# The low-rank decay columns of a fused decoder layer move into the first indexer group

## The chip, the cores and the metric

One core of a Trainium2 chip runs the whole layer as one program. Its engines are TensorE (PE, matrix products, with PEld for its weight loads), VectorE (DVE), ScalarE (ACT), GpSimd (POOL) and SyncE (SP, which here issues the loads). Each engine takes its own instructions in the order in which the program gives them and waits for the others by semaphores. The metric is the device time of one execution in microseconds (us); the kernel before took 1889.96, 1892.20 and 1893.36 us in three runs, so a median of 1892.2 us.

## The reference, cut to what matters

All is float32: 256 tokens, a model width of 2048, one layer. A normed and modulated input h is multiplied by one wide matrix, and the columns of the result are split among the branches:

```python
proj = h @ w_in                                # 2048 x 16984
(g_q, g_k, g_v, g_r, g_lr, d_q, d_k, d_v, i_q, i_k, i_w, gate_a, gate_b) = split(proj)
# widths: 1024 1024 2048 2048 16 2048 2048 2048 512 64 8 2048 2048
log_g = log_sigmoid(g_lr @ gla_gate_up + gla_gate_bias) / 16    # decay of the linear attention
o_a   = gla_chunked(q_a, k_a, v_a, log_g)      # 4 heads; then norm, gain, silu(g_r)
score = sum_h i_w[h] * relu(i_q[h] . i_k / 8)  # indexer: 8 heads of 64, the best 64 keys per query
o_b   = softmax attention over the chosen keys # 16 heads of 128
x     = x + g1 * ((sigmoid(gate_a) * (o_a @ w_branch_gla) + sigmoid(gate_b) * (o_b @ w_branch_dsa)) @ w_merge_out)
x     = x + g2 * swiglu(norm(x)); return final_norm(x)
```

The change concerns g_lr, 16 columns of the projection, and the indexer's 584 columns (i_q, i_k, i_w).

## The kernel before, in words

Weights stream through the core once. A *chunk* (class Mm) is up to four row tiles of 128 of a weight matrix and up to 512 columns. SP loads it into one of three raw buffers. Then `pre_mm` splits it in halves: ACT rounds a half to the float32r part `hi` (L303) and DVE subtracts it from the original, which gives the exact rest `lo` (L305). `main` multiplies: for each row tile and each of two token tiles of 128, three products, activations' `hi` by weights' `hi` (L345), `hi` by `lo` (L346) and `lo` by `hi` (L347). A chunk of four row tiles is 24 products. A *group* is the four chunks of one set of columns; its result is in two PSUM tiles, which the group's `evac` copies out.

`run` goes through the list `items`. After each chunk's products it records the split of the chunk that comes two later (`pres`), then, behind a group's last chunk, the copies out of PSUM, and then it lets three *threads* each take a step, as long as a credit lasts that grows by 3.6 us for a chunk of 512 columns: `qa` is the gated linear attention (GLA), `qb` the transposes of queries and keys, `qc` the indexer's scoring, top-k search and the softmax attention. A step's small products stand on PE behind the chunk, its other work behind the chunk's split on the other engines. Where a later group needs a thread's result, the thread is *drained*: its remaining steps are recorded at once. All engines keep the order so recorded; there is no other scheduler.

Around the change the list is: the first products (q, k, v, r of GLA) in four slices of the depth; `init_end` (rotary tables, buffers of the later stages); the low-rank chunk (class Lr); two indexer groups of 292 columns; then the groups named in `ORDER = "d0 a0 a1 d1 a2 a3 d2 y0 y1 d3 y2 y3"`, in which a *d* is three groups (queries, keys, values of four attention heads), an *a* a gate and a *y* a branch product.

The low-rank chunk is 2048 x 128 columns, of which 16 are needed. Its weights are the stationary operand: for each row tile one product with 512 columns (both parts of h, L327) and one with 256 (L328), 32 in all, so the result is already transposed, ranks by tokens. `lr_evac` adds the two halves (L591, L592) and starts the GLA thread:

```python
            act.copy(lrT[0:16, 0:S], ps[0:16, 0:S])
            dve.tensor_tensor(lrT[0:16, 0:S], lrT[0:16, 0:S], ps[0:16, S:2 * S], ALU.add)
            state["lr"] = True
            qa.add(gla())
```

The GLA thread first transposes q and k (L613), multiplies the low-rank rows by the gate matrix (L628), takes logarithms and a running sum (L646, L650). Then, for each of 4 heads and 4 pairs of block sizes, `prep` has POOL subtract (L663), ACT take exponentials (L667) and DVE multiply (L672), and the next step has PE multiply (L693 to L705, L679). At a head's end come the product with the values (L732 to L734), a scaling by DVE (L737), a sum of squares on ACT (L738), a power on POOL (L218, L219) and a scaling (L766). After the last head 32 transposes (L753), four to a PSUM tile, are split by ACT (L758) and DVE (L759). `psum_aux` has three buffers. `attend(g)` drains GLA when g is 1. The indexer's columns are copied out by `idx_evac` (L797 to L800); the rotation is `rope` on POOL (L779 to L784), L816 and L826 transpose the indexer's queries and keys, L839 to L847 score, L857 and L858 search the top keys. The transposes of attention queries and keys are L944, the first product of an attention head is L973.

Of the kernel before, what the change touches and what calls it, by code (L numbers as in the profile page):

```python
# [16 lines left out]
S = 256  # L17
# [6 lines left out]
RAW_BUFS = 3          # raw chunks of weights in flight  # L24
EARLY_RAWS = 3        # and more of them while the working tiles of later stages are not there yet
HL_BUFS = 4           # halves of split chunks
AHEAD = 2             # chunks split ahead of their products
INIT_KTS = (4, 4, 4, 4)    # row tiles of the slices of the first products
ADA_DONE = 8          # the group of a slice before which the next slice's modulation is loaded and then applied
ADA_LEAD = (0, 2, 4)  # groups by which each slice's pieces of it start early  # L30
MID = 2               # row tile of the last chunk before which the first token tile's norm goes on
# The second norm's steps (512 columns, token tile) after the first two, with p for a half of a split,
# and the steps done before each row tile of the chunks that read them.
NORM_STEPS = "p 01 11 p p 20 21 30 31"
NORM_DONE = "0000 1233 3333 4557 7777 7777"
SLOT = 3.6            # vector engine time for the threads beside a chunk, in us
# [9 lines left out]
class Mm:  # L46
    """A chunk of a weight matrix: nk row tiles of 128, nc columns, for a group of products.

    With defer, the second token tile waits until a later chunk with by_token has done the first one.
    With home, its parts are in the tiles that home makes and not in the ring of all chunks.  # L50
    """

    def __init__(self, w, k0, nk, c0, nc, grp, first, last):
        self.w, self.k0, self.nk, self.c0, self.nc = w, k0, nk, c0, nc
        self.grp, self.first, self.last = grp, first, last
        self.by_token = self.defer = False
        self.home = ()
        self.ahead = AHEAD

# [7 lines left out]
class Lr:  # L67
    pass


class Ada:
    """A piece of w_ada: nj of every partition's 16 rows, nc columns from c0 on of nseg segments."""
# [11 lines left out]
class Thread:  # L84
# [6 lines left out]
    def step(self):  # L91
        """The next step's cost, which it yields, or None at the end."""
        while True:
            if self.cur is None:
                if not self.q:
                    return None
                self.cur = self.q.popleft()
            try:
                return next(self.cur) or 0.0
            except StopIteration:  # L100
                self.cur = None
# [7 lines left out]
def tile_layer(tc, x, c, positions, norm1_gain, norm2_gain, w_ada, b_ada, w_in, gate_up, gate_bias,  # L109
# [3 lines left out]
    with (  # L113
# [42 lines left out]
        # ------------------------------------------------------------ constants and small inputs  # L156
# [36 lines left out]
        # rotary tables  # L193
# [22 lines left out]
        def rstd_of(ss, n, k):  # L216
            """(ss / n + eps) ^ -0.5 in place, k columns."""
# [3 lines left out]
        def mean_of_three(ss):  # L221
            """ss[:, :, 0] becomes the part of mean + eps of the first three of four sums, for last_rstd."""
# [8 lines left out]
        # ------------------------------------------------------------ the stream of weights  # L231
# [22 lines left out]
        def load(it):  # L254
# [4 lines left out]
            if isinstance(it, Mm):  # L259
                it.raw = raw[:, 0:it.nk * it.nc].rearrange("p (k n) -> p k n", k=it.nk)  # L260
                src = it.w[it.k0 * 128:(it.k0 + it.nk) * 128, it.c0:it.c0 + it.nc].rearrange("(k p) n -> p k n", p=128)
            elif isinstance(it, Lr):
                it.raw = raw.rearrange("p (k n) -> p k n", k=KT)
                src = w_in[:, C_LR:C_LR + 128].rearrange("(k p) n -> p k n", p=128)
            else:
# [5 lines left out]
                return  # L271
            sp.dma_start(it.raw, src)
# [15 lines left out]
        def pre_mm(it, rests_last=False):  # L288
            """The float32 chunk into its float32r part and the exact rest, a step for each half."""
            it.hl = []  # L290
            nk, ncol = (KT, 128) if isinstance(it, Lr) else (it.nk, it.nc)
# [21 lines left out]
        def pre(its):  # L313
            """The pieces of its, a step of each in turn: steps of one piece of w_ada depend on each other."""
# [6 lines left out]
        def main(it):  # L321
            if isinstance(it, Lr):
                ps = psum_main()
                for i, (hv, lv) in enumerate(it.hl):
                    for k in range(8):
                        kt = i * 8 + k
                        pe.matmul(ps, hv[:, k], h1[:, kt].rearrange("p a t -> p (a t)"), start=kt == 0, stop=False)  # L327
                        pe.matmul(ps[:, S:2 * S], lv[:, k], h1[:, kt, 0, :], start=False, stop=kt == KT - 1)  # L328
                it.evac(ps)
                return  # L330
# [31 lines left out]
        def run():  # L362
            raws = [it for it in items if not isinstance(it, Call)]
            first = raws.index(lr)
# [34 lines left out]
            def pre_steps(**order):  # L399
                """The next chunk's pieces, a step at a time."""  # L400
# [9 lines left out]
            for it in items:  # L410
# [13 lines left out]
                early_evac = isinstance(it, Mm) and it.last and it.by_token  # L424
# [3 lines left out]
                if isinstance(it, Mm) and it.last and not early_evac:  # L428
# [5 lines left out]
                credit[0] = min(credit[0] + (SLOT * it.nc / 512 if isinstance(it, Mm) else SLOT), 2 * SLOT)  # L434
# [4 lines left out]
        # ------------------------------------------------------------ first norm and its modulation  # L439
# [13 lines left out]
        def mod_columns(ps, n, A, B, bsc, bsh, gain):  # L453
            """A = (1 + scale) * gain and B = shift of n row tiles, from ps = [shift | scale]."""
# [4 lines left out]
        def modulated(kts, h, A, B, temp, on_act, between=None):  # L459
            """The transposed tokens in xs into the parts of h at the row tiles kts."""  # L460
# [14 lines left out]
        def column_sums(blocks, dst):  # L475
            """The sums of blocks [128, 128] over the partitions, a column of dst for each."""
# [7 lines left out]
        def transpose_x():  # L484
            """xs in place into its transposes, tiles [128, 256] for the row tiles; no block is overwritten before it is read."""
# [102 lines left out]
        # ------------------------------------------------------------ gated linear attention  # L588
        def lr_evac(ps):
            lrT = t2("PT")  # L590
            act.copy(lrT[0:16, 0:S], ps[0:16, 0:S])  # L591
            dve.tensor_tensor(lrT[0:16, 0:S], lrT[0:16, 0:S], ps[0:16, S:2 * S], ALU.add)  # L592
# [3 lines left out]

        lr = Lr()
        lr.evac = lr_evac
        items.append(lr)
# [168 lines left out]
        # ------------------------------------------------------------ indexer  # L768
        def rope(v, nh, dh, rot, step):
            """Rotates the first rot of dh in each of nh heads, in place, on both token tiles."""  # L770
# [19 lines left out]
        def idx_evac(g):  # L790
            def f(ps):
                if g == 0:
                    state["iq"] = t4("tm")
                iq = state["iq"]
                for t in range(2):
                    if g == 0:
                        act.copy(iq[:, t, 0:292], ps[t][:, 0:292])  # L797
                    else:
                        act.copy(iq[:, t, 292:512], ps[t][:, 0:220])
                        dve.tensor_copy(ikw[:, t], ps[t][:, 220:292])  # L800
                if g == 1:
                    qb.add(idx_transposes())
# [65 lines left out]
        for g in range(2):  # L868
            add_group(w_in, C_IDX + g * 292, 292, Grp(act_h(h1), idx_evac(g)))

        # ------------------------------------------------------------ sparse attention
# [3 lines left out]
        def seg_start(i):  # L875
            """Before the first piece of a segment: what the last one left is reduced."""
# [496 lines left out]
```

## Time and profile before

| | |
|---|---|
| runs, us | 1889.96, 1892.20, 1893.36 |
| span of the profiled execution, first to last instruction, us | 1885.6 |
| its own time | the page gives the span only; the median of the runs is 6.6 us above it |
| PE busy | 1834.9 us, 97% of the span |
| DVE, ACT, POOL busy | 1286.0, 854.0, 138.3 us |
| mean share of the 16 DMA engines, data queue of SP | 65.5% |
| granted PE clock, mean | 0.995 of full speed |

A time in a row counts from the span's start. In rows of the timeline the columns are start (us), duration (us, of the whole row where it stands for several instructions), engine, line of the kernel, operation, out <- in, shapes, count, and in brackets how long the engine had been idle and what ended it. PE's products overlap in its pipeline, so the distance between two starts, not the duration, is what one costs. A row of a stretch names each engine's busy time and count, the granted clock, and the share and rate of the DMA.

### The profile page before, as it was taken

What the parts mean: (1) busy time and instruction counts of PE and PEld (TensorE: products, weight loads), DVE (VectorE), ACT (ScalarE), POOL (GpSimd) and SP (SyncE); (2) the same over time, 40 slices, a digit from 0 to 9 for tenths busy, and PEclk for the clock granted to TensorE, in tenths of its full rate; (3) what the DMA queues carried; (4) which work ended last, traced back from release to release, by engine and by line L of the source; (5) the groups of instructions that cost most, each with busy time, mean ns of one, the idle gap of its engine ahead of it and who ended that gap; (6) DMA issues with size and microseconds to landing.
All of it is one profiled execution on the core that took longest, in us unless ns stands there. A gap on an engine that the chain in (4) does not pass through costs nothing.

```text
span 1885.6 us, 23215 instructions
## 1 busy us (share of the span) xinstructions
PE 1834.9 (97%) x9148; PEld 1510.9 (80%) x9148; DVE 1286.0 (68%) x1442; ACT 854.0 (45%) x1115; POOL 138.3 (7%) x201
## 2 busy tenths in 40 slices
PE   3999999999999999999999999999999999999998
PEld 3888888777788888888888787888788888888886
DVE  6899865788866678777777656677555444554455
ACT  4554444655645444344344446444333444334443
POOL 0000000543220110200000000000000000000002
PEclk8999999999999999999999999999999999999999
DMA  9998843543444787878888754888555555555553
GB/s 369 387 345 315 282 161 104 182 154 135 150 164 156 270 298 280 300 269 300 305 312 312 275 193 164 318 328 314 178 200 191 189 189 191 186 194 194 185 180 133
DMA packets 198046, 440.84 MB, mean 234 GB/s; under 512 B 7816, under 2 KB 14112, under 8 KB 188848
## 3 DMA queue, kind: packets, MB, share of 16 engines
q1 hardware_dynamic: 196544, 433.69, 65.5%
q10 hardware_dynamic: 1392, 5.66, 0.8%
q8 instruction: 72, 1.18, 0.2%
q14 instruction: 38, 0.31, 0.0%
HBM read 437.22 MB, written 2.10 MB: 233 GB/s over the span
## 4 chain that ended last, share of the span: by engine, by line
PE 78%; issue 12%; DVE 3%; POOL 3%; ACT 2%; DMA 1%; SPq 0%; POOLq 0%; ACTq 0%; DVEq 0%
PE pm L345 25%; PE pm L347 25%; PE pm L346 25%; DVE acc L285 1%; PE pa L1050 1%; DVE lo L305 1%; ACT hi L303 1%; POOL tm L782 1%; POOL rp L783 1%; POOL rp L780 0%; POOL rp L781 0%; PE ph L679 0%; POOL rp L779 0%; DMA raw<-in_w_ada_dram 0%; PE pa L901 0%
## 5 line engine op out<-in xcount | busy, mean ns | idle before, releaser
L305 DVE TENSOR_TENSOR lo<-raw,hi 128x1024 fp32r<-128x1024 f32 (+1 forms) x632 | 768.0, 1225 | 537.1 <-ACT hi L303 536.7
L303 ACT CAST hi<-raw 128x1024 fp32r<-128x1024 f32 (+1 forms) x632 | 652.6, 1041 | 898.8 <-PE pm L347 714.6
L345 PE MATMUL pm<-hi,h 128*128 128x512 f32 (+1 forms) x1784 | 699.0, 392 | 2.2 <-ACT h L464 1.9
L347 PE MATMUL pm<-hi,h 128*128 128x512 f32 (+1 forms) x1784 | 690.5, 387 | 0.0
L346 PE MATMUL pm<-lo,h 128*128 128x512 f32 (+1 forms) x1784 | 689.6, 387 | 0.2 <-DVE lo L305 0.2
L345 PEld LDWEIGHTS pm<-hi,h 128*128 128x128 f32 x1784 | 335.9, 188 | 70.1 <-ACT h L464 2.3
L347 PEld LDWEIGHTS pm<-hi,h 128*128 128x128 f32 x1784 | 335.5, 188 | 68.9 <-DVE h L471 0.2
L346 PEld LDWEIGHTS pm<-lo,h 128*128 128x128 f32 x1784 | 336.0, 188 | 66.1 <-DVE lo L305 0.9
L345 PE MATMUL pm<-hi,gA 128*128 128x512 f32 x608 | 242.1, 398 | 0.0
L347 PE MATMUL pm<-hi,gB 128*128 128x512 f32 x608 | 237.0, 390 | 0.0
L346 PE MATMUL pm<-lo,gA 128*128 128x512 f32 x608 | 236.8, 389 | 0.1
L285 DVE SCALAR_TENSOR_TENSOR acc<-raw,sc,acc 128x2048 f32<-128x2048 f32 (+2 forms) x122 | 218.2, 1789 | 3.5 <-DMA raw<-in_w_ada_dram 2.6
L346 PEld LDWEIGHTS pm<-lo,gA 128*128 128x128 f32 x608 | 114.2, 188 | 25.1 <-issue 1.7
L345 PEld LDWEIGHTS pm<-hi,gA 128*128 128x128 f32 x608 | 114.2, 188 | 24.7 <-issue 1.9
L347 PEld LDWEIGHTS pm<-hi,gB 128*128 128x128 f32 x608 | 114.1, 188 | 24.2
L1274 POOL TENSOR_TENSOR gC<-gC,gr 128x512 f32<-128x512 f32 x3 | 4.9, 1640 | 716.9 <-ACT pm L1272 716.9
L663 POOL TENSOR_TENSOR acc<-gC 128x512 f32<-128x512 f32 x32 | 40.0, 1260 | 34.0 <-DVE acc L672 33.6
L672 DVE TENSOR_TENSOR acc<-gB,acc 128x256 f32<-128x256 f32 x64 | 32.3, 565 | 6.9 <-ACT acc L667 6.8
L779 POOL TENSOR_TENSOR rp<-tm,cos 128x64 f32<-128x64 f32 x18 | 12.2, 677 | 297.8 <-ACT tm L927 180.1
L981 ACT ACTIVATE S<-S,mx 128x128 f32<-128x128 f32 (+1 forms) x32 | 14.3, 448 | 32.8 <-DVE mx L979 32.8
L667 ACT ACTIVATE acc<-acc 128x256 f32<-128x256 f32 x64 | 22.3, 416 | 9.7 <-POOL acc L663 9.6
L345 PE MATMUL pm<-hi,gr 128*128 128x512 f32 x64 | 24.9, 389 | 0.0
(271 smaller groups left out, 1066.6 us busy)
## 6 DMA issues: line engine op xcount, KB each, us to landing
raw<-in_w_in_dram SPq DMA_DIRECT2D x129, 1024.0 KB, 4.9
raw<-in_w_ffn_gate_up_dram SPq DMA_DIRECT2D x88, 1024.0 KB, 4.9
raw<-in_w_ada_dram SPq DMA_DIRECT2D x64, 1024.0 KB, 4.8
raw<-in_w_ffn_down_dram SPq DMA_DIRECT2D x44, 1024.0 KB, 5.2
raw<-in_w_ada_dram SPq DMA_DIRECT2D x64, 512.0 KB, 8.5
raw<-in_w_branch_gla_dram SPq DMA_DIRECT2D x16, 1024.0 KB, 5.3
raw<-in_w_branch_dsa_dram SPq DMA_DIRECT2D x16, 1024.0 KB, 5.3
raw<-in_w_merge_out_dram SPq DMA_DIRECT2D x16, 1024.0 KB, 5.4
```

The source lines that it names most:

```text
L285: dve.scalar_tensor_tensor(a[:, g], it.raw[:, j, g], s, a[:, g], ALU.mult, ALU.add)
L303: act.copy(hv, src)
L305: rests.append(lambda lv=lv, src=src, hv=hv: dve.tensor_sub(lv, src, hv.bitcast(F32)))
L345: pe.matmul(o, a, hv, start=it.first and k == 0, stop=False)
L346: pe.matmul(o, a, lv, start=False, stop=False)
L347: pe.matmul(o, b, hv, start=False, stop=it.last and k == it.nk - 1)
L663: pool.tensor_tensor(d, v, v[:, :, s - 1:s].to_broadcast([128, n, 2 * s]), ALU.subtract)
L667: act.activation(d, d, AF.Exp, scale=(1.0 if u else -1.0) / 16)
L672: dve.tensor_tensor(w, src, d, ALU.mult)
L782: pool.tensor_tensor(a, u[0], u[1], ALU.subtract)
L783: pool.tensor_tensor(u[0], b, co, ALU.mult)
L1050: pe.transpose(ps[:, a * S + t * 128:a * S + t * 128 + 128], src[:, t, (i * 2 + a) * 128:(i * 2 + a + 1) * 128], ident)
```

## The change

The class Lr, its chunk, its load, its split and its 32 products are gone. The two indexer groups now have 300 columns each instead of 292. In the first, columns 0 to 15 are the low-rank columns of w_in and 284 indexer columns follow; a chunk of it is loaded by two loads (`lead`). The second group has the other 300 indexer columns. `idx_evac` of the first group also copies the first 128 columns of both PSUM tiles to SBUF (`lrs`), and a new step on thread `qb`, `lr_start`, transposes them (two transposes), copies 16 rows out and starts the GLA thread. Comments and docstrings are gone too, so line numbers of the changed kernel are 2 to 12 lower.

```diff
@@ load
-                src = it.w[it.k0 * 128:(it.k0 + it.nk) * 128, it.c0:it.c0 + it.nc].rearrange("(k p) n -> p k n", p=128)
-            elif isinstance(it, Lr):
-                it.raw = raw.rearrange("p (k n) -> p k n", k=KT)
-                src = w_in[:, C_LR:C_LR + 128].rearrange("(k p) n -> p k n", p=128)
+                rows = it.w[it.k0 * 128:(it.k0 + it.nk) * 128, :].rearrange("(k p) n -> p k n", p=128)
+                c, nl = it.lead or (0, 0)
+                if nl:
+                    sp.dma_start(it.raw[:, :, 0:nl], rows[:, :, c:c + nl])
+                sp.dma_start(it.raw[:, :, nl:], rows[:, :, it.c0:it.c0 + it.nc - nl])
...
@@ main
-            if isinstance(it, Lr):
-                ps = psum_main()
-                for i, (hv, lv) in enumerate(it.hl):
-                    for k in range(8):
-                        kt = i * 8 + k
-                        pe.matmul(ps, hv[:, k], h1[:, kt].rearrange("p a t -> p (a t)"), start=kt == 0, stop=False)
-                        pe.matmul(ps[:, S:2 * S], lv[:, k], h1[:, kt, 0, :], start=False, stop=kt == KT - 1)
-                it.evac(ps)
-                return
...
-        def lr_evac(ps):
+        def lr_start(lrs):
+            ps = psum_aux()
+            for t in range(2):
+                pe.transpose(ps[:, t * 128:(t + 1) * 128], lrs[:, t], ident)
             lrT = t2("PT")
             act.copy(lrT[0:16, 0:S], ps[0:16, 0:S])
-            dve.tensor_tensor(lrT[0:16, 0:S], lrT[0:16, 0:S], ps[0:16, S:2 * S], ALU.add)
             state["lrT"] = lrT
             state["lr"] = True
             qa.add(gla())
-        lr = Lr()
-        lr.evac = lr_evac
-        items.append(lr)
+            yield 0.2
...
@@ idx_evac
                 if g == 0:
                     state["iq"] = t4("tm")
+                    lrs = t4("mm")[:, :, 0:128]
                 iq = state["iq"]
                 for t in range(2):
                     if g == 0:
-                        act.copy(iq[:, t, 0:292], ps[t][:, 0:292])
+                        act.copy(iq[:, t, 0:284], ps[t][:, 16:300])
+                        dve.tensor_copy(lrs[:, t], ps[t][:, 0:128])
                     else:
-                        act.copy(iq[:, t, 292:512], ps[t][:, 0:220])
-                        dve.tensor_copy(ikw[:, t], ps[t][:, 220:292])
-                if g == 1:
-                    qb.add(idx_transposes())
+                        act.copy(iq[:, t, 284:512], ps[t][:, 0:228])
+                        dve.tensor_copy(ikw[:, t], ps[t][:, 228:300])
+                qb.add(idx_transposes() if g else lr_start(lrs))
...
-            add_group(w_in, C_IDX + g * 292, 292, Grp(act_h(h1), idx_evac(g)))
+            add_group(w_in, C_IDX + g * 284, 300, Grp(act_h(h1), idx_evac(g)))
+            if g == 0:
+                lr_first = items[-KT // 4]
+                for it in items[-KT // 4:]:
+                    it.lead = C_LR, 16
```

PE, behind the four slices of the first products. Before, the low-rank products (L327, L328) and then the first transposes of GLA (L613) stand ahead of the first indexer chunk (L345 to L347, 292 columns):

```order
L327 MATMUL pm_2355<-h_105,hi_2284 128x512
L328 MATMUL pm_2355<-h_105,lo_2285 128x256
L613 MATMUL pa_2405<-cc,gC_107 128x128
L613 MATMUL pa_2405<-cc,gD_108 128x128
...
L345 MATMUL pm_2423<-hi_2318,h_105 128x292
L346 MATMUL pm_2423<-lo_2319,h_105 128x292
L347 MATMUL pm_2423<-hi_2318,h_105 128x292
```

In the changed kernel the last products of the first indexer group (L333 to L335) are followed by the two new transposes (L581, of the copy `mm`), and by the second indexer group:

```order
L333 MATMUL pm_2360<-hi_2425,h_105 128x300
L334 MATMUL pm_2360<-lo_2426,h_105 128x300
L335 MATMUL pm_2360<-hi_2425,h_105 128x300
L581 MATMUL pa_2505<-cc,mm_2500 128x128 x2
L333 MATMUL pm_2510<-hi_2455,h_105 128x300
L334 MATMUL pm_2510<-lo_2456,h_105 128x300
L335 MATMUL pm_2510<-hi_2455,h_105 128x300
```

The GLA transposes now come one chunk into the second indexer group, and the rest of that thread follows them.

POOL, where the keys of the first attention block are rotated (tm, rp: the rotation; acc, gC: the differences of a decay pair). Before, the differences of several pairs stand ahead of each rotation:

```order
L822 COPY mm_2885<-ikw 128x64 x4
L663 TENSOR_TENSOR acc<-gC_2557 128x512 x4
L779 TENSOR_TENSOR rp_2997<-tm_2974,cos 128x64
...
L784 TENSOR_TENSOR tm_2974<-rp_3004 128x4x16
L663 TENSOR_TENSOR acc<-gC_2557 128x512 x6
L779 TENSOR_TENSOR rp_3368<-tm_3355,cos 128x64
```

After, those of the first pair alone stand ahead of the rotation of the keys, and those of the later pairs behind it and behind two selections of the top-k search:

```order
L651 TENSOR_TENSOR acc<-gC_2702 128x512 x2
L767 TENSOR_TENSOR rp_3167<-tm_3154,cos 128x64
...
L772 TENSOR_TENSOR tm_3154<-rp_3174 128x4x16
L840 AFFINE_SELECT S_3181<-bias 128x128
L841 AFFINE_SELECT S_3181<-bias 128x256
L651 TENSOR_TENSOR acc<-gC_2702 128x512 x8
```

What moved is GLA, by about five chunks against the attention's rotations.

PE, at the end of the value group of d1. Before, the last eight of GLA's closing transposes (L753, of `gr`) are followed by the first attention product (L973) and the next chunk; the other 24 stand in three lots of eight ahead of earlier chunks:

```order
L753 MATMUL pa_5058<-cc,gr_111 128x128
L753 MATMUL pa_5058<-cc,gr_112 128x128
L973 MATMUL pa_5068<-fB_4947,fA_4723 128x128
L973 MATMUL pa_5068<-fB_4947,fA_4723 128x256
L345 MATMUL pm_5079<-hi_4978,h_105 128x512
```

After, the last head's product with the values (L720 to L722) is followed by all 32 (L741), eight PSUM tiles, and then by the attention product (L966):

```order
L335 MATMUL pm_4688<-hi_4793,h_105 128x512
L720 MATMUL pa_4942<-gA_109,AT_2355 128x512
L721 MATMUL pa_4943<-gA_109,AT_2355 128x512
L722 MATMUL pa_4943<-gA_110,AT_2355 128x512
L741 MATMUL pa_4961<-cc,gr_111 128x128
L741 MATMUL pa_4961<-cc,gr_112 128x128
...
L741 MATMUL pa_5024<-cc,gr_112 128x128
L966 MATMUL pa_5034<-fB_4857,fA_4532 128x128
```

No weight product stands between them now.

## Rows read from the trace of the kernel before

**Rows 1.** Busy time of each engine in two stretches of 50 us.
```profile
350.00:400.00 50.00, 45.82 (x425) 35.98 (x424) 45.83 (x67) 25.78 (x46) 34.73 (x48) 1.00 0.46 155
400.00:450.00 50.00, 50.00 (x422) 40.10 (x421) 43.78 (x101) 23.73 (x43) 18.68 (x26) 1.00 0.43 148
```

**Rows 2.** Waits of PE, 295 to 760 us: total us, times, longest.
```profile
PE pa L816 <- POOL tm L784: 3.6, 1, 3.6
...
PE pa L826 <- POOL mm L822: 0.6, 1, 0.6
```

**Rows 3.** Timeline of PE around the low-rank products.
```profile
304.86 0.39 PE L345 MATMUL pm<-hi,h 128*128 128x512 f32 x1
...
305.54 0.39 PE L327 MATMUL pm<-h,hi 128*128 128x512 f32 x1
...
311.18 0.27 PE L613 MATMUL pa<-cc,gC 128*128 128x128 f32 x1
311.29 0.27 PE L613 MATMUL pa<-cc,gD 128*128 128x128 f32 x1
```

**Rows 4.** Timeline at the end of an indexer chunk: ACT, PE, DVE.
```profile
319.61 1.26 ACT L303 CAST hi<-raw 128x876 fp32r<-128x876 f32 x2 [2.68 <-PE pm L347]
...
320.21 0.27 PE L613 MATMUL pa<-cc,gC 128*128 128x128 f32 x1
...
320.57 1.44 DVE L305 TENSOR_TENSOR lo<-raw,hi 128x876 fp32r<-128x876 f32 x2 [1.83 <-ACT hi L303]
```

**Rows 5.** Timeline of DVE at GLA's first heads.
```profile
359.01 4.88 DVE L650 TENSOR_TENSOR_SCAN gC<-acc 128x256 f32<-128x256 f32 x8
...
399.90 1.41 DVE L847 SCALAR_TENSOR_TENSOR bias<-S,ikw,bias 128x128 f32<-128x128 f32 x4
...
405.75 1.28 DVE L929 COPY tm<-pm 128x512 f32<-128x512 f32 x2
...
427.66 1.43 DVE L672 TENSOR_TENSOR acc<-gB,acc 128x256 f32<-128x256 f32 x4
```

**Rows 6.** Timeline of PE: one gate step of GLA.
```profile
324.38 1.99 PE L628 MATMUL pa<-PT,fC 16*128 16x256 f32 x8
```

**Rows 7.** The page's costliest group: busy us, mean ns, idle before it.
```profile
L305 DVE TENSOR_TENSOR lo<-raw,hi 128x1024 fp32r<-128x1024 f32 (+1 forms) x632 | 768.0, 1225 | 537.1 <-ACT hi L303 536.7
```

**Rows 8.** Timeline of POOL: rotation of the keys, then a pair's differences.
```profile
406.51 0.33 POOL L779 TENSOR_TENSOR rp<-tm,cos 128x64 f32<-128x64 f32 x1 [12.45 <-DVE tm L929]
...
412.66 0.32 POOL L784 TENSOR_TENSOR tm<-rp 128x64 f32<-128x64 f32 x1
...
414.63 2.11 POOL L663 TENSOR_TENSOR acc<-gC 128x512 f32<-128x512 f32 x2
```

**Rows 9.** Timeline at the end of GLA's last head: PE, DVE, POOL.
```profile
538.57 1.02 PE L732 MATMUL pa<-gA,AT 128*128 128x512 f32 x2
...
540.99 1.28 DVE L737 TENSOR_TENSOR gr<-gr,pa 128x512 f32<-128x512 f32 x2
...
542.18 0.88 DVE L766 TENSOR_SCALAR gr<-gr,ss 128x512 f32<-128x512 f32 x2
...
543.35 0.70 POOL L219 TENSOR_TENSOR ss<-ss,half 128x2 f32<-128x2 f32 x1
```

**Rows 10.** Timeline: splits of two PSUM tiles of closing transposes.
```profile
554.98 0.48 DVE L759 SCALAR_TENSOR_TENSOR gB<-pa,cols,gA 128x256 fp32r<-128x256 f32 x1
555.49 0.84 ACT L758 ACTIVATE gA<-pa,cols 128x256 fp32r<-128x256 f32 x2 [1.31 <-DVE gB L759]
...
556.91 0.47 ACT L758 ACTIVATE gA<-pa,cols 128x256 fp32r<-128x256 f32 x1 [0.58 <-DVE gB L759]
```

**Rows 11.** Busy time of each engine in two stretches of 5 us.
```profile
40.00:45.00 5.00, 5.00 (x16) 3.97 (x15) 4.90 (x7) 1.53 (x2) 0.00 (x0) 0.65 1.05 387
...
355.00:360.00 5.00, 1.41 (x10) 1.01 (x9) 5.00 (x5) 1.04 (x1) 4.76 (x5) 1.00 0.63 210
```

**Rows 12.** Timeline of PE: the first transposes, of the input.
```profile
22.31 0.98 PE L491 MATMUL pa<-cc,gB 128*128 128x128 f32 x4
23.12 0.60 PE L491 MATMUL pm<-cc,gB 128*128 128x128 f32 x4
```

## Prediction of the time after

> **What bounds the kernel now.** I read the table of busy time by stretch first. Between 350 and 450 us TensorE (PE) is busy 45.82 and 50.00 of 50 us, while VectorE (DVE) is at 45.83 and 43.78 [rows 1]: PE sets the time, DVE is close behind, and what PE waits for passes straight to the end, since PE has no slack later to give it back. Second, the waits of PE between 295 and 760 us, where the change lies. They are few: 3.6 us for the indexer's rotation on GpSimd (POOL) and 0.6 us for its key copies are the two that the change can touch [rows 2]. Third, the timelines around four places: the low-rank product, the end of an indexer chunk, the first head of the gated linear attention (GLA), and the place where GLA ends. Order rows come from the two programs, every duration from the trace.
>
> **The change part by part.** *Removed: the low-rank product.* Its 32 products run from 305.54 us to the first transpose behind them at 311.18: 5.64 us, with PE never idle [rows 3]. Its load of 1 MB, two casts and two subtractions lie beside PE's work and are worth nothing by themselves. Gain 5.64.
>
> *Added: 8 columns in each indexer product.* Two groups of 16 row tiles, two token tiles and three products are 192 products. Three 512-column products take 0.68 us (304.86 to 305.54, [rows 3]), 0.227 each or 0.44 ns a column; 192 x 8 x 0.44 ns = 0.68 us. The transposed low-rank block costs two transposes at 0.11 (311.18 to 311.29, [rows 3]), 0.22. Together 0.9.
>
> *Added: a wait in front of those transposes.* They stand directly behind the last product of the first indexer group, and PE takes its work in order: the whole second group is queued behind them. They need DVE's copy of the group's 128 first PSUM columns, and DVE has that copy behind the subtractions of a later chunk. At the same kind of chunk end (PE moves on at 320.21) the casts run from 319.61 and the two subtractions from 320.57 for 1.44, so to 322.01, 1.80 after PE was done [rows 4]. Two copies follow. No row has their size: between nothing and 0.64 each (half of the 1.28 for two 512-column copies, [rows 5]); I take 0.25, nearer to a quarter of the latter. PE waits 2.3 us, bounds 1.8 to 3.1.
>
> *Moved: the GLA thread starts about five chunks later.* Before, it began behind the low-rank product and its steps stood between the indexer's chunks; now its first step comes after the first chunk of the second indexer group. (a) The rotation of the indexer gets more time: two gate steps of 1.99 us each [rows 6] now stand on PE ahead of the transposes that waited 3.6, and the exponentials that held up ScalarE (ACT) there have moved later. Both waits go, 3.6 + 0.6 = 4.2 us; bounds 0 to 4.2.
>
> (b) At GLA's first head the indexer's scoring now stands in the same DVE queue, and the rotation of the keys in the same POOL queue. Count from the end E of the third chunk of the first key group. DVE: subtractions until 2.5 after E (as in [rows 4], with 1.225 each, [rows 7]), the scan 4.88, four scoring steps 1.41, two subtractions 2.45, two copies of the keys 1.28, then the four products of the first decay pair 1.43 [rows 5]: about 13.9. PE arrives after two chunks of 24 x 0.227 = 5.44 and a batch of small products between them (taken as 1.3, between four transposes of 0.11 and a gate step) at 12.2; it needs first one half, then the other, and waits 1.0 to 1.7, say 1.2. Next, the rotation can start only when the first copy of the keys has landed, at 11.9; it takes 6.5 (406.51 to 412.98), two selections some 0.8 (half of the 1.65 from there to 414.63, where other work stood too), and only behind them come POOL's two differences of the next pair, 2.11 [rows 8]: 21.3. With an exponential and a product of about 0.4 each (a quarter of 1.43) it is 22.1. PE arrives at 13.9 + 0.6 + 5.44 = 19.9 and waits 2.2. The remaining two pairs share DVE with the top-k search, which filled DVE to 43.78 of 50 us before [rows 1]: I add 1.6. Sum 5.0. The bounds are 0 (DVE keeps ahead, as in 400 to 450 us, where PE did not wait) and 11 (each of the four pairs waits as long as the longest above with one more subtraction ahead of it, 2.2 + 0.5).
>
> (c) GLA must be finished before the second block of attention heads starts. Before, its 32 closing transposes stood eight at a time between four chunks. Now the last head's product, all 32 transposes and the first attention product stand in one piece, with no weight product among them. Take PE's start there as zero, with the rows of the same head before, 538.57 [rows 9]. PE's own work is 2.57 (six halves of 0.43), 32 x 0.11 = 3.5, and 0.5 for the attention product: 6.5. The chain beside it: DVE could begin scaling at 540.99, 2.42 later; now a copy of 0.64 stands ahead, 3.06. The power on POOL ends at 544.05, another 3.06 later: 6.1; two scalings 0.88: 7.0 [rows 9]. Only then come the splits out of PSUM, and there ACT and DVE take turns on a PSUM tile: ACT's part starts at 555.49 and for the next tile at 556.91, so 1.42 a tile, not the 0.84 of its own two [rows 10]. The first tile is free one such step after 7.0, the sixth after six, at 7.0 + 6 x 1.42 = 15.5. There are three PSUM buffers, and the attention product needs the sixth tile's; with its 0.5 PE is back at 16.0. It was busy for 6.5: a wait of 9.5 us. Bounds: 6.6 if the two engines did not take turns (0.94 a tile, two operations of 0.47, [rows 10], so 7.0 + 6 x 0.94 + 0.5 - 6.5), and 12 if the last head's splits were late by another scaling and a chunk's subtractions.
>
> Sum: -5.64 - 4.2 + 0.9 + 2.3 + 5.0 + 9.5 = +7.9 us, so 1893.5 for the profiled span of 1885.6. The median of the runs shown, 1892.2, is 6.6 above that span (1890.0 to 1893.4 over three runs); I leave this part as it is: 1900.1 us.
>
> **Rivals.** *Not slower: DVE and POOL keep ahead at the first head.* Place: the first decay pair. If DVE's queue is done before 12.2 after E, the 5.0 of (b) vanish and the sum is +2.9: 1895.1, within what a measurement of this kernel can tell from no change, 0.2% or 3.8 us. It decides at (b) below 3.8 - 2.9 = 0.9 us. For it: no PE wait on this product in 400 to 450 us. Against it: there the scoring and the scan did not share the queue.
>
> *Clock lost in the gap of (c).* PE would have 0.44 us of transposes every 1.42 for 8 us. After the long idle at the start the granted clock was 0.65 on the mean of 40 to 45 us, and 16 products began there where at full rate 22 fit (5 / 0.227): 6 x 0.227 = 1.4 us lost there, and as much again before 40 us at most [rows 11]; the attention product and the last closing transposes at half rate add some 0.9: about +3, 1903.1, and up to 1909 with the upper bound of (b). Against it: at 355 to 360 us, with 1.41 us of work in 5, the clock stayed at 1.00 [rows 11]. A rule bears on this: of the Trainium skill, the page "TensorE: Matmul & The Clock Gate", Part 4 (PE-mode transpose), says that transposes do not count as activity for the full clock, which would make the whole gap look idle. This trace differs: within the first transposes, with no product before them, four took 0.98 us in a row at 22.31 and 0.60 at 23.12 [rows 12], so the rate rose on transposes alone.
>
> *The change takes less from the schedule than the order says: faster.* If the splits of (c) ran at 0.94 a tile (6.6) and (b) were zero, the sum is 7.9 - 5.0 - 2.9 = 0.0: 1892.2. For under 1888.4, (c) would have to be below 2.8 us, against three PSUM buffers and the turn-taking of [rows 10].
>
> *The 16 columns come late*, as they are pieces of 64 bytes and a second load per chunk. Four chunks are touched; DMA was at 0.43 to 0.46 of its time here [rows 1], and the loads run three chunks (16 us) ahead. A delay of even 5 us per chunk is covered; 1900.1 stands.
>
> **How the numbers follow.** The forecast (1896 to 1903) has 0.53; the lost clock or a larger (b), 1903 to 1909, 0.17; the first head without cost, 1893.5 to 1896, 0.20; both (b) and (c) small, 1888.4 to 1893.5, 0.06; below that 0.04. So slower by over 0.2% is 0.53 + 0.17 = 0.70, the same 0.20 + 0.06 = 0.26, faster 0.04. The range leaves out a tenth at either end: 1893.5 to 1907.
>
> **What would show it.** In the profile after: no row of the low-rank product; a PE wait of about 2.3 us ahead of the two new transposes; no wait for the indexer's rotation; PE waits for decay products of the first head that sum to 2 to 9 us; and one stretch of 13 to 17 us around the closing transposes, with about 9.5 us of PE idle and PE waiting for DVE's splits. Wrong would be: the closing transposes without idle time, or new waits on loads.

## The result and the profile after

| | before | changed |
|---|---|---|
| median of 5 runs, us | 1891.3 | 1900.35 (1898.4 to 1902.9) |
| ratio | 1 | 1.0052, 95% interval 1.0041 to 1.0063 |
| span of the profiled execution, us | 1885.6 | 1901.1 |

The change makes the kernel slower by 0.5%, 7.7 to 11.9 us. The two spans differ by more, 15.5 us: the profile shown is that of the slowest of the five executions. A second profile of the same kernel (e9, below) has a span of 1894.6, 9.0 above that of before.

PE's waits between 295 and 795 us, the answer to [rows 2] (total us, times, longest):

```profile
PE pa L741 <- DVE gB L747: 4.2, 5, 2.8
PE ph L667 <- DVE acc L660: 2.5, 5, 1.0
PE pa L581 <- issue: 2.0, 1, 2.0
PE pa L681 <- DVE acc L660: 1.9, 1, 1.9
...
PE pa L693 <- DVE acc L660: 1.2, 1, 1.2
PE pa L978 <- ACT pa L726: 1.0, 1, 1.0
```

The two waits of [rows 2] have no successor (the rotation's transposes are L805, L815 now). New are L581 (the transposes of the low-rank block), L681 and L693 (the first head's decay products), L741 (the closing transposes) and L978. L667 had a wait before too, 1.6 us.

In front of the new transposes, DVE and then PE. The columns of a timeline row: start, duration, engine, line, operation, tiles; in brackets the idle time ahead and what ended it:

```profile
319.52 1.48 DVE L302 TENSOR_TENSOR lo<-raw,hi 128x900 fp32r<-128x900 f32 x2 [1.85 <-ACT hi L300]
320.91 0.48 DVE L787 COPY mm<-pm 128x128 f32<-128x128 f32 x2
```
```profile
321.30 0.48 PE L581 MATMUL pa<-cc,mm 128*128 128x128 f32 x2 [1.97 <-issue]
```

The copies stand behind two subtractions of another chunk, as at the chunk end of [rows 4]. PE goes on as they end. The profile names no releaser; the DVE rows do.

The first head's products:

```profile
400.14 0.71 PE L681 MATMUL pa<-acc 128*128 128x128 f32 x4 [1.87 <-DVE acc L660]
401.06 0.68 PE L686 MATMUL pa<-acc 128*64 128x64 f32 x8 [0.21 <-DVE acc L660]
408.63 0.45 PE L693 MATMUL pa<-acc 128*32 128x32 f32 x16 [1.23 <-DVE acc L660]
410.11 0.50 PE L667 MATMUL ph<-acc 128*32 128x32 f32 x32 [1.03 <-DVE acc L660]
```

The end of GLA on PE, from the last head's product to the next chunk:

```profile
566.94 1.02 PE L720 MATMUL pa<-gA,AT 128*128 128x512 f32 x2
...
571.41 1.26 PE L741 MATMUL pa<-cc,gr 128*128 128x128 f32 x8 [1.30 <-ACT pa L726]
575.50 1.09 PE L741 MATMUL pa<-cc,gr 128*128 128x128 f32 x4 [2.83 <-DVE gB L747]
576.92 1.09 PE L741 MATMUL pa<-cc,gr 128*128 128x128 f32 x4 [0.33 <-DVE gB L747]
...
582.59 1.62 PE L966 MATMUL pa<-fB,fA 128*128 128x128 f32 x4 [0.33 <-DVE gB L747]
583.65 0.99 PE L333 MATMUL pm<-hi,h 128*128 128x512 f32 x1
...
586.57 0.48 PE L333 MATMUL pm<-hi,h 128*128 128x512 f32 x1
```

and the same stretch by engine (PE, weight load, DVE, ACT, POOL busy; then the granted clock):

```profile
570.00:575.00 5.00, 1.37 (x10) 0.84 (x8) 3.44 (x9) 2.29 (x7) 0.89 (x2) 0.81 0.65 210
575.00:580.00 5.00, 3.51 (x14) 2.43 (x15) 3.37 (x8) 2.72 (x7) 0.00 (x0) 0.50 0.02 3
...
585.00:590.00 5.00, 5.00 (x20) 4.07 (x19) 2.00 (x5) 2.04 (x5) 0.00 (x0) 0.82 0.00 0
```

PE passes from the last head to the next weight chunk in 16.7 us with 6.5 us of work, counted at the full clock. The tiles come every 1.42 us, as ACT and DVE take turns on them:

```profile
575.78 0.84 ACT L746 ACTIVATE gA<-pa,cols 128x256 fp32r<-128x256 f32 x2 [0.58 <-DVE gB L747]
576.29 0.88 DVE L747 SCALAR_TENSOR_TENSOR gB<-pa,cols,gA 128x256 fp32r<-128x256 f32 x2 [0.54 <-ACT gA L746]
```

The clock falls to 0.50, the lower of the two levels, and stays there into the chunk: from 583.65 its first six products take 2.92 us, where 6 x 0.227 = 1.36 are due, so some 1.5 us are lost there.

### The profile page after: what moved, and what is told of

Read it like the earlier page. It is cut to its first block, busy times and chain, and to the rows that moved or that the text cites. A ratio compares the mean times of both kernels' runs of the same rounds, so it can differ in the third digit from the quotient of the medians.

```text
span 1901.1 us, 23145 instructions
## 1 busy us (share of the span) xinstructions
PE 1840.2 (97%) x9118; PEld 1512.1 (80%) x9118; DVE 1280.0 (67%) x1441; ACT 853.4 (45%) x1113; POOL 122.4 (6%) x201
## 4 chain that ended last, share of the span: by engine, by line
PE 82%; issue 8%; DVE 4%; POOL 2%; ACT 2%; DMA 1%; SPq 0%; POOLq 0%; ACTq 0%; DVEq 0%
PE pm L333 26%; PE pm L335 26%; PE pm L334 26%; DVE acc L282 1%; DVE lo L302 1%; ACT hi L300 1%; PE pa L1043 1%; DMA raw<-in_w_in_dram 1%; DVE acc L660 1%; DMA raw<-in_w_ada_dram 0%; PE pa L894 0%; POOL rp L769 0%; POOL rp L771 0%; POOL tm L770 0%; PE pa L966 0%
## 5 line engine op out<-in xcount | busy, mean ns | idle before, releaser
L333 PE MATMUL pm<-hi,h 128*128 128x512 f32 (+1 forms) x1784 | 699.9, 392 | 2.2 <-ACT h L452 1.9
L335 PE MATMUL pm<-hi,h 128*128 128x512 f32 (+1 forms) x1784 | 691.6, 388 | 0.0
L333 PEld LDWEIGHTS pm<-hi,h 128*128 128x128 f32 x1784 | 336.6, 189 | 70.6 <-ACT h L452 2.3
L335 PEld LDWEIGHTS pm<-hi,h 128*128 128x128 f32 x1784 | 336.0, 188 | 68.9 <-DVE h L459 0.3
L333 PE MATMUL pm<-hi,gA 128*128 128x512 f32 x608 | 242.1, 398 | 0.0
L335 PE MATMUL pm<-hi,gB 128*128 128x512 f32 x608 | 236.9, 390 | 0.0
L333 PEld LDWEIGHTS pm<-hi,gA 128*128 128x128 f32 x608 | 114.2, 188 | 24.6 <-issue 1.9
L335 PEld LDWEIGHTS pm<-hi,gB 128*128 128x128 f32 x608 | 114.1, 188 | 24.0
L767 POOL TENSOR_TENSOR rp<-tm,cos 128x64 f32<-128x64 f32 x18 | 10.8, 598 | 299.8 <-ACT tm L920 198.1
L655 ACT ACTIVATE acc<-acc 128x256 f32<-128x256 f32 x64 | 22.3, 415 | 10.5 <-POOL acc L651 10.3
L333 PE MATMUL pm<-hi,gr 128*128 128x512 f32 x64 | 24.9, 389 | 0.0
```

The source lines that it names most:

```text
L333: pe.matmul(o, a, hv, start=it.first and k == 0, stop=False)
L335: pe.matmul(o, b, hv, start=False, stop=it.last and k == it.nk - 1)
L655: act.activation(d, d, AF.Exp, scale=(1.0 if u else -1.0) / 16)
L767: pool.tensor_tensor(u[0], a, co, ALU.mult)
```

## The experiments

The reference is the kernel before, run beside each of them (medians 1889.2 to 1890.1). Each time below is a median; ratios are to the kernel before, with their intervals.

**e3: the shift of GLA alone, without the change.** The kernel before, in which GLA starts where it starts after the change:

```diff
             state["lrT"] = lrT
+        def gla_start():
             state["lr"] = True
             qa.add(gla())
+            yield 0.2
...
-                if g == 1:
-                    qb.add(idx_transposes())
+                qb.add(idx_transposes() if g else gla_start())
```

> The kernel before, with its low-rank product, its 292 columns and no new transposes; only the start of the GLA thread is put off to where the change puts it. My theory (the shift of GLA is the loss): -4.2 for the rotation waits, +5.1 at the first heads, +11.5 at the end: +12.4 on 1891.3, so 1903.7, 1900 to 1907. Rival: the loss comes from what stands at the front of the change (the wait for the copies, the added columns), and the shift is neutral: 1890 to 1893.

Measured: 1902.9, ratio 1.0068 (1.0056 to 1.0081), so +12.9 us. Its long waits between 295 and 795 us are those of the changed kernel (the three longest):

```profile
PE pa L756 <- DVE gB L762: 4.6, 5, 2.8
PE ph L682 <- DVE acc L675: 2.0, 4, 0.9
PE pa L696 <- DVE acc L675: 1.9, 1, 1.9
```

The shift makes the loss; the front of the change does not. This also shows the net of the terms -4.2, (b) and (c) nearly by itself: 0.5 us in it is a wait of the first indexer chunk (`pm L345 <- DVE PT L592`) that neither of the two kernels has.

**e4: the gain alone.** The kernel before with 2 of 32 low-rank products.

```diff
-                for i, (hv, lv) in enumerate(it.hl):
-                    for k in range(8):
...
+                hv, lv = it.hl[0]
+                pe.matmul(ps, hv[:, 0], h1[:, 0].rearrange("p a t -> p (a t)"), start=True, stop=False)
+                pe.matmul(ps[:, S:2 * S], lv[:, 0], h1[:, 0, 0, :], start=False, stop=True)
```

> The kernel before with 2 of the 32 low-rank products; load, casts and subtractions stay, and so does all of the order; 30 products are left out, so the gate's input is not what it should be. My theory: the 5.64 us are on the path, 30/32 of them go: 5.3 us less than 1891.3, 1886.0, and each later PE wait as before. Rival: a wait behind it, that for the indexer's rotation (3.6 us) above all, takes the gain back: 1889 or more.

Measured: 1883.75, ratio 0.9971 (0.9962 to 0.9981): -5.5 us (-7.2 to -3.6). From the first low-rank product to the first indexer product PE takes 1.58 us here instead of 6.87, so the 5.3 us are gained at the place itself. The rotation's wait is still 3.60 us in its trace, as in [rows 2]. But the expectation that each later wait stays as before was wrong, as a new one stands right behind the gain:

```profile
308.88 0.40 PE L343 MATMUL pm<-hi,h 128*128 128x292 f32 x1 [1.38 <-DVE PT L590]
```

The second token tile of the first indexer chunk waits until DVE has read the low-rank result (L590). PE comes there 5.3 us earlier, but ACT and DVE first finish the rotary tables, which they do until 307.9 us. Of the 5.3 us, 3.1 are left at 656 us in this profile, whose execution took 1888.5 us. The gain is real, and some of it was taken back here; the changed kernel does not have this wait.

**e2: the turns of ACT and DVE.** The changed kernel; per closing tile both of ACT's operations are issued ahead of both of DVE's.

```diff
-                    for a in range(2):
-                        ...
-                        act.mul(hi, ps[:, a * S:(a + 1) * S], g)
-                        dve.scalar_tensor_tensor(lo, ps[:, a * S:(a + 1) * S], g, ...)
+                    for lows in range(2):
+                        for a in range(2):
+                            ...
+                            if not lows:
+                                act.mul(hi, ps[:, a * S:(a + 1) * S], g)
+                            else:
+                                dve.scalar_tensor_tensor(lo, ps[:, a * S:(a + 1) * S], g, ...)
```

> The changed kernel, with the four split operations of each closing PSUM tile issued in another order: both of ACT, then both of DVE, not in turns. My theory (the turns make 1.42 us a tile): the tiles come every 0.94 us, six tiles give 6 x 0.48 = 2.9 us less, 1897.5; if the clock then stays at full rate another 1.9, 1895.6. Rival: ACT and DVE are kept apart on a PSUM tile in any order, or the tile rate is set by something else (the release of the three buffers): within 1 us of 1900.35, and 1.42 us a tile in the trace.

Measured: 1894.1, ratio 1.0018 (1.0009 to 1.0027), 4.3 us below the changed kernel as measured in e9, 6.4 below it as first measured. The same stretch in the trace:

```profile
567.32 1.02 PE L720 MATMUL pa<-gA,AT 128*128 128x512 f32 x2
...
575.24 2.79 PE L741 MATMUL pa<-cc,gr 128*128 128x128 f32 x12 [2.20 <-DVE gB L750]
578.26 1.94 PE L741 MATMUL pa<-cc,gr 128*128 128x128 f32 x8 [0.22 <-DVE gB L750]
579.99 0.99 PE L969 MATMUL pa<-fB,fA 128*128 128x128 f32 x4
580.63 0.58 PE L333 MATMUL pm<-hi,h 128*128 128x512 f32 x1
581.51 0.40 PE L333 MATMUL pm<-hi,h 128*128 128x512 f32 x1
```
```profile
576.36 2.55 ACT L748 ACTIVATE gA<-pa,cols 128x256 fp32r<-128x256 f32 x6 [1.84 <-PE pa L741]
577.24 2.58 DVE L750 SCALAR_TENSOR_TENSOR gB<-pa,cols,gA 128x256 fp32r<-128x256 f32 x6 [0.57 <-ACT gA L748]
```

It is 13.3 us instead of 16.7 (-3.4; -2.9 was expected), and only the first weight product is still slow (another -1.4). Three tiles now take 3.0 us, 1.0 each, so the 1.42 us come from the order in which the program issued the splits. ACT and DVE are still never on one tile at once: DVE begins a tile when both of ACT's operations on it are done, 0.88 us after ACT. In turns, ACT's second half waited for DVE's first, though it takes no data from it; now ACT goes on with the next tile meanwhile. The clock fell here too (0.50 from 575 to 580 us), so my hope that it would not was wrong.

**e7: is it the idle time that takes the clock?** The changed kernel, each closing transpose three times into the same place (`for a in (0, 1) * 3`).

> The changed kernel, with each of the 32 closing transposes done three times over into the same place, so that PE has 1.3 us of work in each 1.42 us of the turns instead of 0.44. Theory A (the clock falls because PE idles there, and that costs 1.9 us): the granted clock stays at 1.00, no half-rate products after the piece: 1898.0 to 1899, although 64 transposes are added. Theory B (it falls in the idle time of the first tiles, or transposes do not keep it up): the 12 transposes take 2.6 us a tile at the half rate, and the piece is 3 to 8 us longer: 1903 to 1908.

Measured: 1894.95, ratio 1.0030 (1.0019 to 1.0041). Adding 64 transposes did not make the kernel slower.

```profile
565.40 1.02 PE L720 MATMUL pa<-gA,AT 128*128 128x512 f32 x2
...
573.95 7.17 PE L741 MATMUL pa<-cc,gr 128*128 128x128 f32 x60 [1.24 <-DVE gB L747]
581.04 0.89 PE L966 MATMUL pa<-fB,fA 128*128 128x128 f32 x4
581.59 0.58 PE L333 MATMUL pm<-hi,h 128*128 128x512 f32 x1
582.47 0.40 PE L333 MATMUL pm<-hi,h 128*128 128x512 f32 x1
```
```profile
570.00:575.00 5.00, 3.76 (x34) 3.55 (x35) 2.90 (x8) 2.39 (x7) 0.89 (x2) 1.00 0.47 181
575.00:580.00 5.00, 5.00 (x45) 4.49 (x43) 3.25 (x8) 2.68 (x8) 0.00 (x0) 1.00 0.00 0
```

The clock stays at 1.00 through 60 transposes, the stretch is 16.2 us (-0.5), and the products behind it run at nearly full rate (-1.5): theory A's 1.9 in the trace. The median is 2 to 4 us (0.11 to 0.22%) below that of the changed kernel, with intervals as wide; 1898 to 1899 was expected. The mean granted clock of whole executions tells the two apart: 0.993 or 0.994 in all seven of this version, 0.989 to 0.992 in all ten of the changed kernel. PE's idle time in the piece fell from 5.8 to 1.7 us, at the first tiles too, so which part of the idle time took the clock is not shown.

**e1: let the closing transposes spread.** The changed kernel, where the second attention block waits only until the buffer that it takes over is free.

```diff
+                        if h == 3 and i == 2:
+                            state["bb"] = True
...
             if g > 0:
-                qa.drain(lambda: "gla" in state)
+                qa.drain(lambda: ("bb" if g == 1 else "gla") in state)
```

> The changed kernel, but the second attention block waits only until GLA has read its decay sums (the buffer that this block takes over), not until GLA is finished; the 32 closing transposes then stand eight at a time between weight chunks again. My theory: the piece of 16.7 us in which PE had 6.5 us of work, and the half clock of 1.35 us behind it, go: 10 to 11.5 us less than the changed kernel's 1900.35, so 1889 to 1890.5, no PE wait on the splits above 1 us, granted clock 1.00 from 560 to 600 us. Rival: the splits of the closing transposes cost the same wherever they stand, because ACT and DVE are then shared with the heads of the attention: at most 4 us less, 1896 or more.

Measured: 1897.0, ratio 1.0039 (1.0027 to 1.0052). The rival was right:

```profile
580.22 1.03 PE L743 MATMUL pa<-cc,gr 128*128 128x128 f32 x8
581.10 0.82 PE L968 MATMUL pa<-fB,fA 128*128 128x128 f32 x4
584.35 0.52 PE L980 MATMUL pa<-cc,S 128*128 128x128 f32 x3 [2.43 <-DVE gB L749]
...
591.77 1.04 PE L743 MATMUL pa<-cc,gr 128*128 128x128 f32 x8
...
603.87 0.87 PE L980 MATMUL pa<-cc,S 128*128 128x128 f32 x3 [4.06 <-DVE gB L749]
```

Eight closing transposes and an attention step behind one chunk need four PSUM tiles of the three; the fourth waits for the splits, and the granted clock is 0.66 in the 5 us from 585. The lot at 591.77, with no attention step beside it, waits for nothing. In the kernel before, a chunk stands between each lot and the next such transposes of an attention head (L980 here, of S).

**e8: three of the five chunks back.** The changed kernel, with GLA started at the end of the first stage; its gates still wait for the low-rank rows.

```diff
+        items.append(Call(lambda: qa.add(gla())))
...
-            qa.add(gla())
             yield 0.2
...
+            while "lrT" not in state:
+                yield 0.0
             bb = g8("gC")
```

> The changed kernel, with only the start of the GLA thread put back to the end of the first stage: its three lots of transposes run beside the first indexer group, the gates still wait for the low-rank columns, and no steps are merged. 24 of the 32 closing transposes are left in one piece. My theory: the piece costs 2 tiles of 1.42 us less and the first heads lose less than 5.1; 3 to 6 us below 1900.35: 1894 to 1897. Rival: the place of the low-rank columns' wait and the added columns matter more than the shift: within 1.5 us of 1900.35.

Measured: 1894.3, ratio 1.0023 (1.0014 to 1.0033), as expected.

**e5: all five back.** e8 and e2 together, and four GLA steps made two (the yields inside the gate loop and inside the exponential loop are moved behind them).

> The changed kernel with the five chunks given back: the GLA thread starts at the end of the first stage again, its three lots of transposes run before the low-rank columns are there, the two gate steps are one and so are the two exponential steps; the split order of the last kernels is kept. The closing transposes stand eight at a time between four chunks again. My theory (the loss is the shift alone): what stays of the change is -5.64 for the product, +1.1 for columns and transposes, +2.0 for the wait, and none to all of the 4.2 of the rotation: -2.6 to -6.8 on 1890.0, so 1883 to 1887.5. Rival: the change itself is no gain, because what it frees on PE is waited for at the splits, the scoring or the key rotation: 1889 to 1892.

Measured: 1886.85, ratio 0.9982 (0.9974 to 0.9991), and again (e10) 1884.3, 0.7 us below what was expected of the repeat, 0.9979 (0.9967 to 0.9991): this version beats both kernels. What the merged steps alone would give the kernel before was not run; the new split order has no wait to remove there, as PE waits for none of its closing transposes. 

> The kernel with the five chunks given back, again, to stand beside the next one: 1885 to 1889.

 Its waits from 295 to 795 us (e10):

```profile
PE pa L581 <- issue: 2.0, 1, 2.0
PE pa L682 <- DVE acc L661: 1.7, 1, 1.7
...
PE pa L819 <- POOL mm L815: 0.8, 1, 0.8
PE pa L687 <- DVE acc L661: 0.8, 1, 0.8
```

The closing transposes stand eight at a time again, without a wait. By these rows: -5.64 + 1.2 (columns, transposes) + 2.0 + 2.5 (L682, L687) - 3.4 (4.2 less the 0.8 left) = -3.3, against -3.4 and -4.0 by the ratios; counted from the end of the first products, the trace of e10 is 3.5 us ahead of that of the kernel before at 652 us. The trace of e5, the same program with the same waits, is only 0.3 ahead. It loses the other 3.2 between the wait at L581 and the first attention group, where PE is never idle but runs at a lower granted clock. From 330 to 335 us the clock is 0.68 in e5 and 1.00 in e10; the next 5 us, e5 and then e10:

```profile
335.00:340.00 5.00, 5.00 (x26) 5.00 (x25) 0.07 (x1) 1.14 (x3) 0.00 (x0) 0.64 0.08 32
```
```profile
335.00:340.00 5.00, 5.00 (x38) 5.00 (x37) 4.61 (x4) 4.80 (x6) 0.00 (x0) 1.00 0.40 129
```

The clock fell in this stretch in the profiles of e6 and e11 too, so single profiles of these versions differ by as much as the edits.

**e6: one step more merged, the new transposes one chunk later.**

> As the kernel before it in this call, with the two Silu steps made one as well, and with the two new transposes put off by one chunk, so that PE no longer waits for the copies of the low-rank columns. GLA is then one chunk later again: 16 of its 32 closing transposes stand in one piece. My theory: the wait of 2.0 us goes, and a piece of 16 costs less than 2: 1882 to 1888. Rival: the later GLA costs more than the hidden wait gives: 1 to 3 us above the kernel beside it.

Measured: 1891.6, ratio 1.0008 (0.9997 to 1.0018), 4.7 us above e5, more than the rival's 1 to 3: the wait at L581 went, and two larger ones came. One is `L743 <- DVE gB L752`, 2.6 us, at the piece of 16; the other:

```profile
363.48 6.52 DVE L640 TENSOR_TENSOR_SCAN gC<-acc 128x256 f32<-128x256 f32 x8
369.92 0.39 DVE L822 COPY PT<-pa 128x256 f32<-128x256 f32 x1
```
```profile
370.37 1.66 PE L833 MATMUL pa<-PT,mm 64*128 64x128 f32 x8 [3.78 <-DVE PT L822]
```

GLA's scan now stands ahead of the copy of the indexer's keys, which PE needs for scoring.

**e11: the wait of L581.** e5, with the first indexer group's copies issued ahead of the next chunk's split.

> The kernel with the five chunks given back, and the copies of the first indexer group now issued ahead of the next chunk's casts and subtractions instead of behind them; PE's order stays word for word. My theory (the wait in front of the two new transposes is DVE's two subtractions of 1.44 us): the wait falls from 1.97 to 0.4 to 0.9, and the time by 1.0 to 1.5 against the kernel beside it. Rival: the subtractions that now stand behind the copies are late for the next group's products, and PE waits there for the same time: no difference.

Measured: PE's wait at L581 is 0.40 us, named `DVE mm L791` now: the two subtractions were the wait. The time is 1884.1 beside e10's 1884.3, ratio 0.9973 (0.9962 to 0.9983); the difference of the two is inside their intervals, so whether 1.5 us reach the end stays open. Its profile can't settle it, as it loses more to the clock (0.85, 0.50 and 0.96 in the three stretches of 5 us from 325 us) than the shorter wait gives, beside that of e10 (1.00).

**e9: the changed kernel again.**

> The changed kernel itself once more, for a second profile. If the late wait for the rotation of the keys near 812 us (3.5 us, and half the clock for six products behind it, against 2.46 before) belongs to the change, it is there again and the time at the end of this profile is 14 to 16 us above that of before; if it is scatter between executions, the wait is 1 to 2.6 us, and the end is 9 to 12 us above.

Measured: 1896.6, ratio 1.0041 (1.0029 to 1.0054). The late wait of the first profile (`L937`, 0.71 and 2.80 us near 812 us, granted clock 0.66 behind it) is 1.22 us here, the clock stays at 1.00. It is scatter, not the change.

## Why the prediction was right

The forecast was +7.9 us; the two comparisons gave +9.8 and +7.7 (0.52% and 0.41% of some 1890). That 1900.1 stands so near 1900.35 is luck: the base was taken 0.9 too high, and the second comparison gave 1896.6. Step by step:

- *The product, -5.64:* right. Its rows are gone, and e4 shows 5.3 for 30 of the 32 products at their place; its time, -5.5, agrees within a wide interval.
- *Rotation and key copies, -4.2:* right, both rows are gone.
- *Columns and transposes, +0.9:* three products of 300 columns take 0.415 us in the changed trace, three of 292 took 0.40, so 64 x 0.015 = 1.0, and 0.24 for the transposes: 1.2.
- *The wait in front of them, +2.3:* 1.97, for the reason given (e11).
- *(b), +5.0:* the first pair waits 2.1 (1.2 expected), the second 2.3 (2.2). In e9 PE runs the chunk between the two at a granted clock of 0.66 and the second pair waits only 0.7, but PE goes on at the same time after the first pair (9.9 us), so the chain over POOL, ACT and DVE sets this point, as worked out. The remaining two pairs wait 0.4 (1.6 expected). The later heads, for which I had put nothing, wait 1.0, and 1.0 more at L978 for a PSUM tile that GLA holds, which I had not seen. The sum is 6.8, but 1.6 of it replaces the wait that the kernel before had at the same product, which I did not subtract: net 5.2. That 5.0 comes so near is partly luck.
- *(c), +9.5:* the chain is as worked out. The sixth tile is free at 582.59, 15.65 us after the start (15.5 expected). The piece is 16.7 instead of 16.0, because the attention product runs at half rate, and 1.5 us are lost behind it: 10.2 + 1.5 = 11.7. The sign of 9.5 us of idle PE did not come: PE's idle time in the piece is 5.8 us, as its transposes ran at half rate in the rest.

The measured terms sum to -5.64 - 4.2 + 1.2 + 2.0 + 5.2 + 11.7 = +10.3. The traces differ by 11.3 us near 640 us (10.8 in e9), 0.35 of it from ahead of the change.

What I judged wrongly was the rival of the lost clock, at 0.17. It happened, in each of the changed kernel's two profiles, and cost 2.0 us, not 3. The row I held against it, the clock at 1.00 with 1.41 us of work in 5 [rows 11], could not carry that: it holds the wait of 3.6 us of [rows 2], longer than any single wait of (c), and in e4 the same wait was followed by a clock of 0.66. The rule of the Trainium skill that I weighed there is "TensorE: Matmul & The Clock Gate", Part 4, PE-mode transpose: transposes do not count as activity for the full clock. It does not agree with e7, where 7 us of nothing but transposes ran at 1.00 and threefold work kept the clock that single work lost.

## What to carry to other kernels

When a product is taken off a full engine, ask what its place in the order held: here the low-rank product was where a long side thread got its data, and 5.6 us of products were bought with five chunks of that thread's lead. A thread that must be finished by a given point has a lead that can be counted in the order before anything is run; where the lead is gone, its whole rest lands on the bottleneck engine in one piece, at the pace at which its PSUM tiles come free (here 1.42 us each). Give the lead back (start the parts that don't need the data, merge cheap steps) before judging the saving.

## What the runs showed of the hardware

- Superfluous transposes can pay: with 64 more of them the granted clock stayed at 1.00, the piece and the products behind it took 1.9 us less in the trace, and the median was 2 to 4 us lower, at the edge of its interval.
- ACT and DVE kept off each other's PSUM tile in the closing splits, and the order in which their operations were issued decided what that cost: 1.42 us a tile in turns, 1.0 with both of ACT's first.
- The same wait at the same product is followed by a lower clock in one run and not in another. At the indexer's rotation PE waits 3.6 us in the kernel before [rows 2] and in e4. The 5 us behind the wait, first in the kernel before and then in e4 (same columns as above):

```profile
360.00:365.00 5.00, 5.00 (x25) 4.14 (x24) 5.00 (x10) 1.05 (x1) 4.45 (x13) 1.00 0.61 210
```
```profile
355.00:360.00 5.00, 4.58 (x17) 3.77 (x18) 5.00 (x10) 0.00 (x0) 4.61 (x10) 0.66 0.63 210
```

  In the same way the clock stays at 1.00 behind 2.46 us of idle time at the rotation near 800 us in the kernel before, and is 0.66 behind 2.43 us in e1; and in the two profiles of one program, e5 and e10, it fell once and once not. Why is open.
- Executions of one kernel differ by several us. The rotation's wait near 800 us was 1.2 in one profile of the changed kernel and 3.5 in another, and no edit touched it. In e10 the time of an execution goes with its mean granted clock: 1882.1 to 1883.0 us at 0.994 or 0.995, 1885.7 at 0.992, 1888.7 to 1892.3 at 0.990.
